# First modulation of a two-block network: weights fetched ahead of the constants, and its last 512 columns computed with the weights as stationary operand

## Chip, cores and metric

The kernel runs on one core of a Trainium2 chip, as one launch. The metric is the device time of that launch in microseconds (us); lower is better. A profile of one execution lists every instruction with its start and length. PE is TensorE's matmul stream, PEld its weight loads, DVE is VectorE, ACT is ScalarE, POOL is GpSimd, SP is SyncE, whose queue issues every DMA here.

## What is computed

A two-layer block (an mLSTM mixer, a gated spatial mixer, a feed-forward network after each), followed by a block with sparse attention, a convolution branch and 16384 small experts, for 256 tokens of width 1024. All of it is float32. The change touches only how the first layer's modulation vectors are made:

```python
c_act = jax.nn.silu(c)                        # c: 1 x 1024
for i in range(DEPTH):
    mod = c_act @ ada_w[i] + ada_b[i]         # 1 x 6144
    sh1, sc1, g1, sh2, sc2, g2 = jnp.split(mod[:, None, :], 6, axis=-1)
    h = rmsnorm(x, norm_g[i, 0]) * (1.0 + sc1) + sh1
    ...                                       # mixer (mLSTM for i = 0), residual, ffn
```

`sh1` and `sc1` of layer 0 are needed before the first projection can start; the other four vectors are made in the background, between other work.

## The kernel before

The program is written for a tile framework: code names tiles and engines, and a scheduler sets the order of each engine's instructions from priorities. Inside an engine's list nothing overtakes. All DMAs are issued by SP, in one list.

`full` calls `setup` and then `first_block`. `setup` (L339) issues three constant loads: `cols` (331 columns of small vectors, `c` among them), `kc` (six 128x128 matrices: identity, ones, masks) and `ciota`; then it makes `cact` = silu(c), 8 columns of 128 values.

`first_block` (L866) first spreads `cact` over 128 columns (`crep`, L871) and makes `sh1` and `sc1` in four blocks of 512 output columns with `ada_start` (L494). A block needs 8 chunks of weights, 128 rows by 512 columns each. They come as four DMAs of 512 KB, two to a staging tile `st` (pool `wst`, three tiles of 1 MB). Even chunks go to PE: `crep[:, kk]` is the stationary operand and the 512 weight columns move (L512), so that all 128 rows of the result are equal. Odd chunks are multiplied and summed on DVE into `s` (L508, L510), and one matmul with the ones matrix (L513) adds that sum over the partitions. `diagonal` (L517) takes the wanted column form out of the 128 equal rows with two DVE operations over 512 columns (L521, L522), L515 adds the bias, and L877 forms (1 + sc1) * gain after the last block. X is fetched behind the first block's weights (L875).

`Finish.whole` (L247) then normalises X (`chain`, L157), transposes it on PE (`turn`, L194, L203), scales it with `sc1` and `sh1` on DVE (L212, first half of the features) and ACT (L216, second half) into `hf`, and runs the heads (L128): the gate weights (40 columns, `a_w_g`) and the first two of the query/key column groups, for each half of the tokens (`t` = 0, 1), with L135. The tiles for these head weights take the room of `crep`. What follows is `mlstm` (L625): six query/key groups with `dense_b` (L407, its matmuls on L397 to L399), meanwhile the gate chain on ACT and DVE (L639 to L661: `th`, `lf`, `C`, `av`, `M`, `em`), then the value projection with `Acc.emit` (L113) from `a_w_v`, and background work from `self.side`: the other modulation vectors by `ada_block` (L524, its DVE steps on L538).

Weights for `dense_b` and `Acc` arrive in float32 and are split: ACT makes `hi` (L365), DVE makes `lo` (L366).

Of the kernel before, what the change touches and what calls it, by code (L numbers as in the profile page):

```python
# [10 lines left out]
F32 = mybir.dt.float32  # L11
# [5 lines left out]
AF = mybir.ActivationFunctionType  # L17
ALU = mybir.AluOpType
# [5 lines left out]
KD = 8  # L24
T = 256
EPS = 1e-6
NEG = -1.0e30
# [248 lines left out]
class Net:  # L276
# [61 lines left out]

    def setup(self):  # L339
        nc, c, a = self.nc, self.const, self.a  # L340
        self.cols = c.tile([128, NCOL], F32, name="cols")
        nc.sync.dma_start(self.cols, a["cols"])
        self.X = self.keep.tile([128, 2, D], F32, name="X")
        k = c.tile([128, 6, 128], F32, name="kc")
        nc.sync.dma_start(k, a["k128"])
        self.junk = self.const.tile([128, D], BF16, name="junk")
        self.ident, self.ones, self.mbig, self.anti, self.bdiag, self.iota = (k[:, i] for i in range(6))
        self.cand_iota = c.tile([128, NCAND], F32, name="ciota")
        nc.sync.dma_start(self.cand_iota, a["ciota"])
        self.mhalf = c.tile([128, 1], F32, name="mhalf")  # L350
        nc.gpsimd.memset(self.mhalf, -0.5)
        self.eps = c.tile([128, 1], F32, name="eps")
        nc.gpsimd.memset(self.eps, EPS)
        self.cact = c.tile([128, KD], F32, name="cact")
        nc.scalar.activation(self.cact, self.col("c"), AF.Silu)

    def col(self, name, i=None, n=1):
        at, w = COLS[name]
# [132 lines left out]
        return t  # L491


    def ada_start(self, i, b, o):  # L494


        nc = self.nc
        s = self.ada_p.tile([128, 1024], F32, tag="ada", name="ada")[:, :512]
        w = self.a["ada_w"][i, b // 2].rearrange("q p (k n) -> q p k n", k=2)[:, :, :, (b % 2) * 512:(b % 2 + 1) * 512]
        ps = self.sd_tile()  # L500
        for h in range(2):
            st = self.wst.tile([128, 2048], F32, tag="st", name="st").rearrange("p (k n) -> p k n", k=4)
            for q in range(2):
                nc.sync.dma_start(st[:, 2 * q:2 * q + 2], w[2 * h + q])
            for k in range(4):
                kk = 4 * h + k
                if kk == 1:
                    nc.vector.tensor_scalar(s, st[:, k], self.cact[:, kk:kk + 1], None, op0=ALU.mult)  # L508
                elif k % 2:
                    nc.vector.scalar_tensor_tensor(s, st[:, k], self.cact[:, kk:kk + 1], s, op0=ALU.mult, op1=ALU.add)  # L510
                else:
                    nc.tensor.matmul(ps, self.crep[:, kk], st[:, k], start=kk == 0, stop=False)  # L512
        nc.tensor.matmul(ps, self.ones, s, start=False, stop=True)  # L513
        self.diagonal(ps, o)
        nc.vector.tensor_tensor(o, o, self.col("ada_b", 48 * i + 4 * b, 4), op=ALU.add)  # L515

    def diagonal(self, ps, o):  # L517

        nc = self.nc
        d = self.ada_p.tile([128, 4, 128], F32, tag="adad", name="adad", bufs=1)  # L520
        nc.vector.tensor_tensor(d, ps.rearrange("p (k c) -> p k c", k=4), self.ident.unsqueeze(1).to_broadcast([128, 4, 128]), op=ALU.mult)  # L521
        nc.vector.tensor_reduce(o, d, axis=AX.X, op=ALU.add)  # L522
# [343 lines left out]
    def first_block(self):  # L866
        with self.tc.tile_pool(name="adap", bufs=2) as self.ada_p, self.tc.tile_pool(name="wsx", bufs=2) as self.wsx:
            m0, first, rest = self.ada_mods(0)
            with self.tc.tile_pool(name="crep", bufs=1) as p:
                self.crep = p.tile([128, KD, 128], F32, name="crep")  # L870
                self.nc.vector.tensor_copy(self.crep, self.cact.unsqueeze(2).to_broadcast([128, KD, 128]))  # L871
                for b in range(4):
                    self.ada_start(0, b, m0["sh1" if b < 2 else "sc1"][:, 4 * (b % 2):4 * (b % 2) + 4])
                    if b == 0:
                        self.nc.sync.dma_start(self.X, self.a["x"].rearrange("o (t p) d -> p (o t) d", p=128))  # L875
                o = m0["sc1"]
                self.nc.vector.scalar_tensor_tensor(o, o, 1.0, self.col("ng0_0"), op0=ALU.add, op1=ALU.mult)  # L877
            with self.tc.tile_pool(name="st0", bufs=2) as p, self.tc.tile_pool(name="work", bufs=1) as work:
                fin = Finish(self, work, None, m0["sc1"], m0["sh1"], head=[(self.a["a_w_g"], 1, 40)] + self.pairs(self.a["a_w_qk"], 2), head_pool=p)
                fin.whole()  # L880
            self.side = rest[:3]
            x = self.mlstm(fin.x, 2.0, lambda p, hst: Finish(self, p, m0["g1"], m0["sc2"], m0["sh2"], head=self.pairs(self.a["ffn_w1"][0], 4), head_pool=hst))
            m1, first, rest1 = self.ada_mods(1)
            with self.tc.tile_pool(name="sgc", bufs=1) as p:
                self.side = rest[3:] + first + [self.sgu_setup(p)]
                with self.tc.tile_pool(name="hst1", bufs=1) as hst:
                    x = self.ffn(x, 0, Finish(self, None, m0["g2"], m1["sc1"], m1["sh1"], head=self.pairs(self.a["b_w_u"], 4), head_pool=Both(hst, self.wst)), 3.2)
                self.side = rest1[:3]

                rows = Lent(self.sgu_c[:2])  # L890
                x = self.sgu(x, 1.2, lambda v: Finish(self, None, m1["g1"], m1["sc2"], m1["sh2"], head=self.pairs(self.a["ffn_w1"][1], 3), head_pool=rows, space=v))
            self.side = rest1[3:]
            with self.tc.tile_pool(name="hst2", bufs=2) as hst:
                x = self.ffn(x, 1, Finish(self, None, m1["g2"], self.col("attn_g"), head=self.pairs(self.a["w_glu"], 3), head_pool=hst), 2.0)
        self.wsx = None
        return x
# [605 lines left out]
def prep(i):  # L1502
    c = lambda v: np.asarray(v).reshape(-1, 128).T
# [9 lines left out]
    for l in range(2):  # L1513
        for j in (0, 2):
            col[f"ng{l}_{j}"] = c(i["norm_g"][l, j])
    o = {}
    o["cols"] = np.concatenate([col[n] for n in COLS], axis=1)
    p, f = np.arange(128)[:, None], np.arange(128)[None, :]
    f32 = np.float32
    o["k128"] = np.stack([  # L1520
        (p == f).astype(f32), np.ones((128, 128), f32), np.where(p > f, f32(-NEG), f32(0)), (p + f == 127).astype(f32),
        (p // 64 == f // 64).astype(f32), np.broadcast_to(f.astype(f32), (128, 128)),
    ], axis=1)
    o["ciota"] = np.broadcast_to(np.arange(NCAND, dtype=f32)[None], (128, NCAND))
# [6 lines left out]
    w = i["a_w_in"][0]  # L1531
# [5 lines left out]
    w = i["b_w_in"][0]  # L1537
# [5 lines left out]
    w = i["w_in_2"][0]  # L1543
# [37 lines left out]
```

## Time and profile before

| | us |
|---|---|
| median of 3 runs | 1751.74 |
| lowest, highest run | 1751.68, 1752.71 |
| profiled execution, its own time | 1752.71 |
| its span, first to last instruction | 1751.0 |
| PE busy in the span | 1713.6 (98%) |

The 1.7 us between the profiled execution's time and its span lie before the first and behind the last instruction. Rows of the timeline give the start, the length, engine, line, operation, tiles and count of a run of equal instructions; in brackets stands how long the engine was idle before them and what ended that idle time. A float32 matmul appears as two records on PE. The next two sections show the change and the rows.

### The profile page before, as it was taken

Reading aid. Unit: us, or ns where it says so; the run is one execution under the profiler, and the core shown is the slowest. Engines: PE = TensorE matmul, PEld = TensorE weight load, DVE = VectorE, ACT = ScalarE, POOL = GpSimd, SP = SyncE. Lnnn points to the kernel's source line nnn. Section 1 sums busy time; section 2 is a strip of 40 time slices with the busy share of each in tenths; the row PEclk is TensorE's granted clock in tenths of the full one; section 3 lists DMA queues with packets and bytes.
Section 4 is the critical chain, followed back from the end, with each engine's and each line's share of the span. In section 5 each row is a group of like instructions: output and inputs, shape, how many; then the busy total and the mean of one; then the engine's idle time right before and its main releaser. Section 6 shows DMA issues by size and latency. Waiting matters only on the chain.

```text
span 1751.0 us, 28455 instructions
## 1 busy us (share of the span) xinstructions
PE 1713.6 (98%) x11306; PEld 1511.8 (86%) x11306; DVE 1382.8 (79%) x2407; ACT 917.0 (52%) x1519; POOL 31.7 (2%) x43
## 2 busy tenths in 40 slices
PE   7999999999999999999999999999999999999998
PEld 3878888877888888999999999999888998787886
DVE  6787996578959655999767999799788948888754
ACT  3565566544546665666555445445444444445543
POOL 0010000000000000000000000000000000000000
PEclk9999999999999999999999999999999999999999
DMA  9876887367818653444355555544554455554751
GB/s 341 307 283 243 332 320 295 121 219 286 309 65 334 211 191 129 152 169 147 119 180 182 174 188 184 178 165 165 177 172 168 167 173 189 176 184 160 258 192 45
DMA packets 59599, 352.42 MB, mean 201 GB/s; under 512 B 6165, under 2 KB 12613, under 8 KB 19273
## 3 DMA queue, kind: packets, MB, share of 16 engines
q1 hardware_dynamic: 59466, 350.61, 56.7%
q8 instruction: 88, 1.44, 0.3%
q14 instruction: 45, 0.37, 0.1%
HBM read 349.51 MB, written 1.07 MB: 200 GB/s over the span
## 4 chain that ended last, share of the span: by engine, by line
PE 85%; DVE 8%; DMA 2%; issue 2%; ACT 2%; POOL 1%; SPq 0%; POOLq 0%; DVEq 0%; ACTq 0%
PE acc L113 38%; PE mm L397 10%; PE mm L399 10%; PE mm L398 10%; PE mm L426 6%; PE mm L428 3%; PE head L135 3%; DVE lo L366 2%; DVE yc L937 1%; DMA st<-in_b_w_v_dram 1%; PE sd L1234 1%; PE sd L1245 1%; DVE ada L538 1%; PE sd L512 1%; DMA st<-in_ada_w_dram 1%
## 5 line engine op out<-in xcount | busy, mean ns | idle before, releaser
L365 ACT CAST hi<-st 128x1024 fp32r<-128x1024 f32 (+1 forms) x507 | 525.9, 1049 | 435.7 <-PE mm L398 196.0
L366 DVE TENSOR_TENSOR lo<-st,hi 128x1024 fp32r<-128x1024 f32 (+1 forms) x507 | 613.1, 1221 | 153.0 <-ACT hi L365 151.2
L397 PE MATMUL mm<-h,hi 128*128 128x256 f32 x1544 | 443.2, 287 | 0.7 <-ACT qz L670 0.7
L399 PE MATMUL mm<-h,lo 128*128 128x256 f32 x1544 | 436.7, 283 | 1.9 <-DVE lo L366 1.9
L398 PE MATMUL mm<-h,hi 128*128 128x256 f32 x1544 | 436.9, 283 | 0.0
L399 PEld LDWEIGHTS mm<-h,lo 128*128 128x128 f32 x1544 | 295.2, 191 | 2.6 <-DVE lo L366 2.6
L397 PEld LDWEIGHTS mm<-h,hi 128*128 128x128 f32 x1544 | 295.4, 191 | 1.9 <-ACT qz L670 0.9
L398 PEld LDWEIGHTS mm<-h,hi 128*128 128x128 f32 x1544 | 295.5, 191 | 0.2
L113 PE MATMUL acc<-hi,h 128*128 128x512 f32 x768 | 232.0, 398 | 6.6 <-ACT hi L365 4.7
L113 PEld LDWEIGHTS acc<-hi,h 128*128 128x128 f32 x768 | 143.1, 190 | 37.9 <-ACT hi L365 6.2
L113 PE MATMUL acc<-lo,h 128*128 128x512 f32 x544 | 172.1, 394 | 0.2
L426 PE MATMUL mm<-h,hi 128*128 128x512 f32 x456 | 161.6, 399 | 0.0
L113 PE MATMUL acc<-hi,vh 128*128 128x512 f32 x448 | 142.5, 399 | 0.0
L113 PE MATMUL acc<-lo,vh 128*128 128x512 f32 x448 | 138.7, 391 | 0.0
L113 PE MATMUL acc<-hi,vl 128*128 128x512 f32 x448 | 138.0, 389 | 0.0
L113 PEld LDWEIGHTS acc<-lo,h 128*128 128x128 f32 x544 | 102.2, 189 | 23.7 <-DVE lo L366 2.5
L428 PE MATMUL mm<-h,lo 128*128 128x256 f32 x399 | 111.9, 281 | 0.0
L113 PEld LDWEIGHTS acc<-hi,vl 128*128 128x128 f32 x448 | 84.1, 188 | 18.4
L113 PEld LDWEIGHTS acc<-lo,vh 128*128 128x128 f32 x448 | 84.1, 188 | 18.1
L538 DVE SCALAR_TENSOR_TENSOR ada<-st,cact,ada 128x1024 f32<-128x1024 f32 x74 | 94.7, 1280 | 5.7 <-DMA st<-in_ada_w_dram 3.3
L113 PE MATMUL acc<-hi,l 128*128 128x512 f32 x320 | 99.0, 389 | 0.0
L426 PEld LDWEIGHTS mm<-h,hi 128*128 128x128 f32 x456 | 83.7, 188 | 16.6 <-issue 0.5
(398 smaller groups left out, 2198.7 us busy)
## 6 DMA issues: line engine op xcount, KB each, us to landing
st<-in_peer_u_dram SPq DMA_DIRECT2D x64, 1024.0 KB, 4.9
st<-in_peer_v_dram SPq DMA_DIRECT2D x64, 1024.0 KB, 4.9
st<-in_ffn_w_dram SPq DMA_DIRECT2D x62, 1024.0 KB, 5.7
st<-in_ada_w_dram SPq DMA_DIRECT2D x40, 1024.0 KB, 6.2
st<-in_ada_w_dram SPq DMA_DIRECT2D x16, 512.0 KB, 6.2
st<-in_b_w_u_dram SPq DMA_DIRECT2D x8, 1024.0 KB, 5.0
st<-in_b_w_v_dram SPq DMA_DIRECT2D x8, 1024.0 KB, 4.9
st<-in_b_w_out_dram SPq DMA_DIRECT2D x8, 1024.0 KB, 5.2
```

Of the source, the lines that this page charges most:

```text
L113: ins = mm(self.t[t][j], a[:, ts], b[:, j * 512:(j + 1) * 512], start=first and a is xh and b is wh, stop=last and a is xl)
L135: net.nc.tensor.matmul(ps[:, t * 128:(t + 1) * 128], w[:, k], x(k), start=k == 0, stop=k == KD - 1)
L365: i = self.nc.scalar.copy(hi, src)
L366: return i.ins, self.nc.vector.tensor_tensor(lo, src, hi.bitcast(F32), op=ALU.subtract).ins
L397: mm(out, ahi, bhi, start=start, stop=False)
L398: mm(out, ahi, blo, start=False, stop=False)
L399: return mm(out, alo, bhi, start=False, stop=stop)
L426: i = mm(ps, wh[:, k], x2[:, k], start=first, stop=last)
L428: i = mm(ps[:, :T], wl[:, k], xh[:, k], start=False, stop=False)
L512: nc.tensor.matmul(ps, self.crep[:, kk], st[:, k], start=kk == 0, stop=False)
L538: nc.vector.scalar_tensor_tensor(s, w, c, s, op0=ALU.mult, op1=ALU.add)
L937: nc.vector.scalar_tensor_tensor(y[:, n], up[:, n, w:w + T], self.col("conv_w", n * 31 + w), y[:, n], op0=ALU.mult, op1=ALU.add)
```

## The change

`setup` now loads only `c` (8 columns, tile `c8`). The identity and ones matrices, X and `cols` are issued by `fetch`, which `ada_start` calls after the first block's first two weight DMAs; the remaining matrices (`kd`, three of them, since an unused one is dropped) and `ciota` are issued by `fetch_more`, after `Finish.whole`. The fourth block goes through the new `ada_last`: its 8 chunks come as eight DMAs of 256 KB, each 128x128 part of a chunk is loaded as stationary operand, and one column of `cact` moves (L545 of the new kernel), 32 matmuls with one column of output each, summed over the chunks in four PSUM tiles; four DVE operations on single columns (L547) add bias and one and multiply by the gain.

```diff
     def setup(self):
         nc, c, a = self.nc, self.const, self.a
+        c8 = c.tile([128, KD], F32, name="c8")
+        nc.sync.dma_start(c8, a["cols"][:, :KD])
         self.cols = c.tile([128, NCOL], F32, name="cols")
-        nc.sync.dma_start(self.cols, a["cols"])
...
+    def fetch(self):
+
+        nc, a = self.nc, self.a
+        nc.sync.dma_start(self.k2, a["k128"][:, :2])
+        nc.sync.dma_start(self.X, a["x"].rearrange("o (t p) d -> p (o t) d", p=128))
+        nc.sync.dma_start(self.cols, a["cols"])
+
+    def fetch_more(self):
+
+        nc, a = self.nc, self.a
+        nc.sync.dma_start(self.k4, a["k128"][:, 2:])
+        nc.sync.dma_start(self.cand_iota, a["ciota"])
...
+            if h == 0:
+                then()
...
+    def ada_last(self, i, b, o, ng):
+
+        nc = self.nc
+        b1 = self.small.tile([128, 4], F32, tag="b1", name="b1", bufs=1)
+        nc.vector.tensor_scalar(b1, self.col("ada_b", 48 * i + 4 * b, 4), 1.0, None, op0=ALU.add)
+        w = self.a["ada_w"][i, b // 2].rearrange("q p (k n) -> q p k n", k=2)[:, :, :, (b % 2) * 512:(b % 2 + 1) * 512]
+        ps = [self.acc_p.tile([128, 512], F32, tag="acc", name="adac")[:, :1] for _ in range(4)]
+        for h in range(2):
+            st = self.wst.tile([128, 2048], F32, tag="st", name="st").rearrange("p (k n) -> p k n", k=4)
+            for k in range(4):
+                kk = 4 * h + k
+                nc.sync.dma_start(st[:, k], w[kk // 2, :, kk % 2])
+                for j in range(4):
+                    nc.tensor.matmul(ps[j], st[:, k, j * 128:(j + 1) * 128], self.cact[:, kk:kk + 1], start=kk == 0, stop=kk == KD - 1)
+        for j in range(4):
+            nc.vector.tensor_scalar(o[:, j:j + 1], ps[j], b1[:, j:j + 1], ng[:, j:j + 1], op0=ALU.add, op1=ALU.mult)
...
-                for b in range(4):
-                    self.ada_start(0, b, m0["sh1" if b < 2 else "sc1"][:, 4 * (b % 2):4 * (b % 2) + 4])
-                    if b == 0:
-                        self.nc.sync.dma_start(self.X, self.a["x"].rearrange("o (t p) d -> p (o t) d", p=128))
-                o = m0["sc1"]
-                self.nc.vector.scalar_tensor_tensor(o, o, 1.0, self.col("ng0_0"), op0=ALU.add, op1=ALU.mult)
+                o, ng = m0["sc1"], self.col("ng0_0")
+                self.ada_start(0, 0, m0["sh1"][:, :4], self.fetch)
+                self.ada_start(0, 1, m0["sh1"][:, 4:])
+                self.ada_start(0, 2, o[:, :4])
+                self.nc.vector.scalar_tensor_tensor(o[:, :4], o[:, :4], 1.0, ng[:, :4], op0=ALU.add, op1=ALU.mult)
+                self.ada_last(0, 3, o[:, 4:], ng[:, 4:])
...
                 fin.whole()
+                self.fetch_more()
```

The order of instructions moves at three places that matter below. The first is SP's list at the start of the program; before:

```order
L342 DMA cols<-in_cols_dram 128x331
L345 DMA kc<-in_k_dram 128x768
L349 DMA ciota<-in_ciota_dram 128x54
L504 DMA st<-in_ada_w_dram 128x2x512 x4
L875 DMA X<-in_x_dram 128x2x1024
L504 DMA st<-in_ada_w_dram 128x2x512 x12
L371 DMA st<-in_a_w_qk_dram 128x2048
L371 DMA st<-in_a_w_g_dram 128x320
```

and after the change, where `c` is `c8` and `kc` holds two matrices:

```order
L342 DMA c_84<-in_cols_dram 128x8
L517 DMA st<-in_ada_w_dram 128x2x512 x2
L360 DMA kc<-in_k_dram 128x256
L361 DMA X<-in_x_dram 128x2x1024
L362 DMA cols<-in_cols_dram 128x331
L517 DMA st<-in_ada_w_dram 128x2x512 x10
L543 DMA st<-in_ada_w_dram 128x512 x8
L384 DMA st<-in_a_w_g_dram 128x320
L384 DMA st<-in_a_w_qk_dram 128x2048
L367 DMA kd<-in_k_dram 128x384
L368 DMA ciota<-in_ciota_dram 128x54
```

One small load and two weight pieces now stand ahead of X, X stands ahead of the third piece, and the head weights follow the last modulation piece directly.

The second place is PE's list from the third block to the heads; before:

```order
L512 MATMUL sd<-st,crep 128x512 x2
L513 MATMUL sd<-ada,kc 128x512
L203 MATMUL sd<-kc,xn 128x128 x4
L135 MATMUL head<-hf,st 40x128 x8
L135 MATMUL head<-hf,st 128x128 x16
L135 MATMUL head<-hf,st 40x128 x8
L135 MATMUL head<-hf,st 128x128 x16
```

and after (L527 and L528 are the former L512 and L513):

```order
L527 MATMUL sd<-st,crep 128x512 x2
L528 MATMUL sd<-ada,kc 128x512
L545 MATMUL adac<-cact,st 128x1 x12
L203 MATMUL sd<-kc,xn 128x128 x4
L545 MATMUL adac<-cact,st 128x1 x20
L135 MATMUL head<-hf,st 40x128 x8
L135 MATMUL head<-hf,st 128x128 x16
L135 MATMUL head<-hf,st 40x128 x8
L135 MATMUL head<-hf,st 128x128 x16
```

The fourth block is now a stretch of 32 one-column matmuls, broken only by four transposes, and the heads follow it with nothing between.

The third place is ACT's list in the first mixer, while the query/key groups run on PE (`qz` takes a query group out of PSUM, `hi` splits the last query/key weights); before:

```order
L365 CAST hi<-st 128x1024 x2
L669 COPY qz<-mm 64x256
L670 COPY qz<-mm 64x256
L662 ACT_TABLE_LOAD
L662 ACTIVATE em<-em 8x256
L672 ACTIVATE kT<-mm 128x256 x2
```

and after:

```order
L694 ACT_TABLE_LOAD
L694 ACTIVATE em<-em 8x256
L701 COPY qz<-mm 64x256
L702 COPY qz<-mm 64x256
L378 CAST hi<-st 128x1024 x2
L704 ACTIVATE kT<-mm 128x256 x3
```

The two casts moved behind `em`. DVE's `lo` of the same weights and two background steps wait behind them, and the tile that those steps free is the one into which the first `a_w_v` weights go. From the end of the first mixer on, the lists of all engines are the same as before.

## Rows read from the trace of the kernel before

**Rows 1.** The page: busy time of each engine, share of the span, instructions.
```profile
PE 1713.6 (98%) x11306; PEld 1511.8 (86%) x11306; DVE 1382.8 (79%) x2407; ACT 917.0 (52%) x1519; POOL 31.7 (2%) x43
```

**Rows 2.** Timeline of the start: start us, length, instruction, count, idle before it.
```profile
0.80 0.39 SPq L342 DMA_DIRECT2D cols<-in_cols_dram  x1
...
2.19 2.61 SPq L504 DMA_DIRECT2D st<-in_ada_w_dram  x4
...
3.41 0.70 DVE L871 COPY crep<-cact 128x1024 f32<-128x1024 f32 x1 [3.41 <-ACT cact L355]
4.83 0.63 SPq L875 DMA_DIRECT2D X<-in_x_dram  x1
...
7.02 6.26 PE L512 MATMUL sd<-st,crep 128*128 128x512 f32 x8 [7.02 <-DMA st<-in_ada_w_dram]
```

**Rows 3.** Busy time by stretch: us, engines, granted clock, DMA share, GB/s.
```profile
6.00:20.00 14.00, 10.72 (x21) 4.40 (x22) 7.55 (x14) 3.28 (x9) 1.64 (x2) 1.00 1.04 393
20.00:24.00 4.00, 3.70 (x9) 1.44 (x8) 2.83 (x7) 0.00 (x0) 0.00 (x0) 1.00 0.98 318
```

**Rows 4.** Timeline: third block's last matmul, then the end of the fourth block.
```profile
26.02 1.02 PE L513 MATMUL sd<-ada,kc 128*128 128x512 f32 x2
...
30.73 0.75 DVE L510 SCALAR_TENSOR_TENSOR ada<-st,cact,ada 128x512 f32<-128x512 f32 x1 [0.44 <-DMA st<-in_ada_w_dram]
...
32.70 0.69 DVE L521 TENSOR_TENSOR adad<-sd,kc 128x512 f32<-128x512 f32 x1 [1.22 <-PE sd L513]
...
34.55 2.90 ACT L216 ACTIVATE hf<-mm,sh,sc 128x128 f32<-128x128 f32 x8 [5.21 <-DVE sc L877]
```

**Rows 5.** Timeline of the heads and the first query/key matmul behind them.
```profile
35.02 13.26 PE L135 MATMUL head<-hf,st 128*40 128x128 f32 x96 [0.91 <-DVE hf L212]
...
38.15 6.10 PEld L135 LDWEIGHTS head<-hf,st 128*128 128x128 f32 x48 [0.37 <-issue]
...
44.44 3.65 PEld L135 LDWEIGHTS head<-hf,st 128*128 128x128 f32 x32 [0.19 <-issue]
...
48.03 0.36 PE L397 MATMUL mm<-h,hi 128*128 128x256 f32 x1
```

**Rows 6.** Single lines: ns minimum/median/maximum of a record, first and last start.
```profile
L953 PEld LDWEIGHTS sd<-kc,qi x16: 186/192/192, 852.1 to 853.8; 128*128 128x128 f32 x16
L953 PE MATMUL sd<-kc,qi x16: 250/250/271, 852.1 to 853.8; 128*128 128x1 f32 x16
...
L963 PEld LDWEIGHTS sd<-dg,kc x4: 285/333/333, 855.4 to 856.0; 128*128 128x128 f32 x4
...
L512 PE MATMUL sd<-st,crep x32: 592/593/1191, 7.0 to 31.2; 128*128 128x512 f32 x32
```

**Rows 7.** Busy time by stretch around two falls of the granted clock.
```profile
32.80:36.10 3.30, 1.74 (x11) 1.00 (x12) 3.16 (x9) 1.55 (x5) 0.00 (x0) 1.00 0.96 325
36.20:39.50 3.30, 3.30 (x16) 2.77 (x15) 2.50 (x7) 3.30 (x9) 0.00 (x0) 0.50 0.93 390
...
851.90:855.30 3.40, 3.30 (x28) 3.04 (x27) 0.82 (x4) 1.19 (x2) 0.70 (x1) 1.00 0.20 84
855.40:858.70 3.30, 3.30 (x15) 3.30 (x16) 2.87 (x5) 1.28 (x1) 0.00 (x0) 0.50 0.02 5
```

**Rows 8.** First mixer: issue with its landing (KB, us), then timeline rows.
```profile
st<-in_a_w_v_dram SPq DMA_DIRECT2D x1, 1024.0 KB, 4.9
...
56.96 0.34 SPq L371 DMA_DIRECT2D st<-in_a_w_v_dram  x1
...
57.45 1.28 ACT L662 ACT_TABLE_LOAD   x1
...
66.82 0.63 PE L113 MATMUL acc<-hi,h 128*128 128x512 f32 x2
73.00 0.73 PE L113 MATMUL acc<-hi,h 128*128 128x512 f32 x2 [0.55 <-ACT hi L365]
...
116.50 0.70 PE L695 MATMUL sd<-qz,kT 128*128 128x256 f32 x2 [1.50 <-DVE sh L550]
```

More of the change, by code (lines that the diff above doesn't have):

```diff
@@ L340, in setup @@
         nc, c, a = self.nc, self.const, self.a
+        c8 = c.tile([128, KD], F32, name="c8")
+        nc.sync.dma_start(c8, a["cols"][:, :KD])
         self.cols = c.tile([128, NCOL], F32, name="cols")
-        nc.sync.dma_start(self.cols, a["cols"])
         self.X = self.keep.tile([128, 2, D], F32, name="X")
-        k = c.tile([128, 6, 128], F32, name="kc")
-        nc.sync.dma_start(k, a["k128"])
+        self.k2, self.k4 = c.tile([128, 2, 128], F32, name="kc"), c.tile([128, 3, 128], F32, name="kd")
         self.junk = self.const.tile([128, D], BF16, name="junk")
-        self.ident, self.ones, self.mbig, self.anti, self.bdiag, self.iota = (k[:, i] for i in range(6))
+        self.ident, self.ones = (self.k2[:, i] for i in range(2))
+        self.mbig, self.bdiag, self.iota = (self.k4[:, i] for i in range(3))
         self.cand_iota = c.tile([128, NCAND], F32, name="ciota")
-        nc.sync.dma_start(self.cand_iota, a["ciota"])
         self.mhalf = c.tile([128, 1], F32, name="mhalf")
@@ L354, in setup @@
         self.cact = c.tile([128, KD], F32, name="cact")
-        nc.scalar.activation(self.cact, self.col("c"), AF.Silu)
+        nc.scalar.activation(self.cact, c8, AF.Silu)
+    def fetch(self):
[7 more added lines that the diff above has]
+        nc.sync.dma_start(self.cand_iota, a["ciota"])
     def col(self, name, i=None, n=1):
@@ L491, in bcast_row, with ada_start @@
         return t
-    def ada_start(self, i, b, o):
+    def ada_start(self, i, b, o, then=lambda: None):
         nc = self.nc
@@ L1520, in prep @@
     o["k128"] = np.stack([
-        (p == f).astype(f32), np.ones((128, 128), f32), np.where(p > f, f32(-NEG), f32(0)), (p + f == 127).astype(f32),
+        (p == f).astype(f32), np.ones((128, 128), f32), np.where(p > f, f32(-NEG), f32(0)),
         (p // 64 == f // 64).astype(f32), np.broadcast_to(f.astype(f32), (128, 128)),
```

## Prediction

> **What bounds the kernel now.** I read the page's busy times first: PE is 98% busy over the span [rows 1], so a change of 1% of the time has to be sought where PE waits. The timeline of the start shows one such place. PE's first matmul comes at 7.02, released by a weight DMA [rows 2], and until the features `hf` start at 34.55 the program makes one modulation after the other at the speed of the weight stream: 393 GB/s with the DMA engines full from 6 to 20, 318 GB/s from 20 to 24 [rows 3]. In the tail of the fourth block the reader should see a chain on two engines: the last piece is used at 30.73, PE's ones matmul has ended at 32.70, and DVE's diagonal, bias and gain end at 34.5 [rows 4]. From 35.0 PE is filled: heads until 48.03 (I call this moment H: the first `dense_b` matmul), then query/key groups until 66.82, then `a_w_v` [rows 5, 8]. Instruction order behind the first mixer does not change, so what the change is worth is how far H moves, plus what the first mixer adds or gives back.
>
> **The stream starts earlier: a gain.** Ahead of the first 512 KB piece stood 165.5, 384 and 27 KB of constants; it was issued at 2.19 and used at 7.02 [rows 2], 4.8 later. Now only `c8` is ahead, and one issue takes about 0.45 (the 0.39 of the first one and the gap behind it), so the piece is issued at 1.25. On an idle queue 1024 KB landed 4.9 after their issue [rows 8]; at 393 GB/s they need 2.7, so 2.2 is fixed, and 512 KB need 2.2 + 1.3 = 3.5. It lands at 4.8, 2.2 earlier; if it still takes 4.8, at 6.0, 1.0 earlier. I take 2.1, since the constants that it waited for are gone. `crep` took until 4.1 [rows 2] and its source now lands first, so it isn't late. Against that the identity and ones matrices (128 KB) and `cols` (165.5 KB), which went through before the stream was full, are now inside it: 0.30 MB at 393 GB/s, 0.8. Net -1.3 (ends -0.2 and -1.3).
>
> X now stands ahead of pieces 3 and 4: PE has two pieces early, then waits some 2 us, and works longer at the half clock of the start, where a 512-column record took up to 1191 ns against 593 [rows 6]. Its staging tiles come free later, which is what the 318 GB/s stretch shows today [rows 3]. I price it at +0.4, between 0 and 1.0 (the whole 20 to 24 dip is worth (393 - 318)/393 x 4 = 0.8). Before, PE was through the third block at 26.02 + 2 x 0.43 = 26.9, with 0.43 the spacing of full-clock records in that block. Now it is at S = 26.9 - 1.3 + 0.4 = 26.0, ends 25.6 and 27.7.
>
> **The fourth block: from the DMA's pace to PE's.** Removed are four 512-column matmuls, the ones matmul, DVE's four multiplies and the diagonal: from the use of the last piece at 30.73 to the features at 34.55, 3.8 of chain [rows 4]. Put in their place are 32 one-column matmuls, 64 records, each with its own 128x128 float32 weight load, and four transposes stand among them: 68 records. The trace has this form once: L953, one column, 16 records between 852.1 and 853.8 [rows 6], (853.8 - 852.1)/15 = 0.113 each. So the stretch needs 68 x 0.113 = 7.7 of PE at full clock, while the last DMA lands around 29: PE, not the stream, now sets the end. At full clock it ends at E = 26.0 + 7.7 = 33.7; with 0.4 for the drain and DVE's small operations `sc1` is ready at 34.1. The 3.8 of chain that went away buys 0.4.
>
> **The clock is the term that decides.** The granted clock fell from 2.4 to 1.2 GHz at 36.1, 3.4 after the last dense matmuls had ended [rows 4, 7], and again at 855.3, 3.2 after L953 began; in that stretch PE and PEld were both filled (3.30 and 3.04 of 3.40), and L953 made up 1.8 of it [rows 6, 7]. So one-column matmuls did not hold the clock there, although PE looked busy. In the new version they last over 7 us, and I expect the fall 3.3 after S (I allow 2 to 5; two cases are no rule). At half clock 16 head records took 3.30 [rows 7], 0.21 each, and a weight load 333 ns against 192 [rows 6]; I price the one-column records at 0.21 there. By the fall 3.3/0.113 = 29 records are done; 39 x 0.21 = 8.2 remain: E = 26.0 + 3.3 + 8.2 = 37.5. A fall after 2 gives 38.7, after 5 36.0.
>
> **From E to H.** The heads start at half clock. Both stays at half clock above lasted 3.4 [rows 7], and at the start it took about 5 (eight records in 6.26 instead of 8 x 0.43) [rows 2]; I take 4.3 of dense heads until it rises. 16 records of 40 columns at 0.21 are 3.4 (the first four chunks no longer wait for `sc1`, ACT brings the others in time at 2.90/8 = 0.36 each [rows 4]); 4 more records at 0.21; then 28 + 16 + 32 at full clock, 0.112 each (3.65 for 32 [rows 5]), 8.5. H = E + 12.8 = 50.3, against 48.03: +2.3, ends +0.5 and +3.9 with the fall and the rise alone. The head weights are not in the way: they were issued late before (heads went on at 38.15 [rows 5]), now directly behind the last piece, and land around 32. `fetch_more` is 219 KB on a queue that then has slack; I price it at nothing, and 0.6 (219 KB at 393 GB/s) if it delays the weights behind it.
>
> **The first mixer.** In ACT's list the two `hi` casts of the last query/key weights now stand behind the table load (1.28 [rows 8]) and `em`. By ACT's times before, they end near H + 11; DVE's two `lo` and two background steps behind them end near H + 14.9, and only then the first `a_w_v` can be issued. It was issued at 56.96, H + 8.9; with 4.9 to landing and 1.05 for its cast PE gets it at H + 20.9, where it wants it at 66.82 = H + 18.8 [rows 8]: 2.1 of waiting. The 0.55 that PE waited for the second piece at 73.00 goes. Later PE waits 1.50 for DVE at 116.50 [rows 8], which can absorb part. I take +1.0, ends 0 and +2.0.
>
> Sum: +2.3 + 1.0 = +3.3 on the profiled execution, 1752.7 + 3.3 = 1756.0. That execution lay 1.0 above the median of 1751.7, so the median becomes 1755.0.
>
> **A rule against the trace.** The clock terms above rest on the load's 333 ns at half clock against 192. The Trainium skill (TensorE: Matmul & The Clock Gate, section "LDWEIGHTS (loading the stationary operand)") gives a load's time as its columns divided by 1.2, in ns, 107 for 128 columns, with no term for the clock's state. The 0.113 at full clock agrees; at half clock the rows speak against it. By that page the one-column stretch would not slow down at all, which is the second rival.
>
> **Rivals.** (1) Slower: the clock falls early, 2 after S, and the `a_w_v` wait comes in full. E = 38.7, H = 51.5, +3.5; +2.0 in the mixer: +5.5, 1757.2. It decides if the fall comes within about 2.5 of the start of the one-column stretch. For it: the transposes and DMA-paced matmuls before S are not dense either. Against: the two falls came 3.2 and 3.4 after.
> (2) Loads don't slow at half clock. E = 33.7, the heads still begin at half clock, H = 46.5, -1.5; with +1.0 in the mixer -0.5: 1751.2. Against: 333 ns against 192.
> (3) Faster: weight loads hold the clock. E = 33.7; the last four 40-column chunks wait for ACT until E + 2.3; then 80 records at 0.112, 9.0: H = 45.0, -3.0; +1.0: -2.0, 1749.7, or 1748.7 if the mixer adds nothing. Against: the fall at 855.3 with PEld filled.
>
> **How the numbers follow.** Forecast 0.48 (1755.0, its own range 1752.8 to 1757.2); rival 1 0.25; rival 2 0.17; rival 3 0.10. A measurement of this kernel tells 0.2%, 3.5 us, from no change. Slower by more: most of rival 1 (0.21) and the upper third of the forecast (0.14), 0.35. Faster by more: the low end of rival 3 and of the stream's start, 0.08. The rest, 0.57, is within. The range reaches from rival 3 to the upper end of rival 1 with S late: 1749.0 to 1758.5.
>
> **What would show it.** In the profile of the changed kernel the first matmul stands near 5; the third block's last matmul ends near 26; L545 then runs at 0.11 a record with the DMA ahead of it and, some 3 us in, at 0.21, with the granted clock at 0.50 from there into the heads; the first `dense_b` matmul stands near 50; PE waits some 2 us before its first `a_w_v` matmul. If L545 keeps 0.11 to its end, rivals 2 or 3 hold, told apart by the clock column. If S is off by more than 1.5, the stream's start was mis-priced.

## Result and profile after

| | before | after |
|---|---|---|
| median, us | 1752.71 | 1762.23 |
| lowest, highest run | 1751.68, 1755.13 | 1761.51, 1766.09 |
| span of the profiled execution | 1751.0 | 1760.5 |

The ratio after to before is 1.0061, with a 95% interval of 1.0046 to 1.0076: the change costs 0.6%. It went the way that was forecast, but the time lies 3.7 above the upper end of the range. The kernel of before has 1752.71 over the five runs made beside the changed one; the three runs of its own section had 1751.74.

The page's row of busy times, against [rows 1]: PE is busy 7.7 longer, and its waits grow by 1.8. Busy time grows at half clock too, as the table by stretch below shows.

```profile
PE 1721.3 (98%) x11360; PEld 1522.9 (87%) x11360; DVE 1381.1 (78%) x2405; ACT 917.2 (52%) x1519; POOL 32.7 (2%) x43
```

The timeline of the start of the changed kernel, which answers to [rows 2, 4, 5]:

```profile
1.25 1.29 SPq L517 DMA_DIRECT2D st<-in_ada_w_dram  x2
...
6.22 3.75 PE L527 MATMUL sd<-st,crep 128*128 128x512 f32 x4 [6.22 <-DMA st<-in_ada_w_dram]
...
12.25 2.08 PE L527 MATMUL sd<-st,crep 128*128 128x512 f32 x2 [2.28 <-DMA st<-in_ada_w_dram]
...
22.66 0.66 PE L203 MATMUL sd<-kc,xn 128*128 128x128 f32 x4
...
27.71 1.02 PE L528 MATMUL sd<-ada,kc 128*128 128x512 f32 x2
...
28.57 2.73 PE L545 MATMUL adac<-cact,st 128*128 128x1 f32 x24
...
31.64 7.88 PE L545 MATMUL adac<-cact,st 128*128 128x1 f32 x40
...
39.45 12.87 PE L135 MATMUL head<-hf,st 128*40 128x128 f32 x96
...
52.07 0.36 PE L410 MATMUL mm<-h,hi 128*128 128x256 f32 x1
```

The first matmul is 0.8 earlier, but behind two pieces PE waits 2.28 for the third. The one-column stretch takes 24 records in 2.73 and then 40 in 7.88. The table by stretch says why (us, PE, PEld, DVE, ACT, POOL, granted clock, DMA share, GB/s):

```profile
28.50:32.30 3.80, 3.80 (x36) 3.73 (x34) 3.07 (x8) 0.00 (x0) 0.00 (x0) 1.00 1.04 386
32.40:39.40 7.00, 7.00 (x34) 7.00 (x33) 0.82 (x3) 0.81 (x2) 0.00 (x0) 0.50 1.01 400
39.50:42.50 3.00, 3.00 (x16) 2.67 (x16) 1.79 (x6) 3.00 (x8) 0.00 (x0) 0.50 0.83 273
...
71.00:74.30 3.30, 0.07 (x2) 0.04 (x1) 0.99 (x2) 3.30 (x9) 0.00 (x0) 0.85 1.01 410
74.30:80.10 5.80, 5.80 (x14) 4.54 (x15) 5.76 (x5) 2.85 (x3) 0.00 (x0) 0.50 0.65 233
```

From 32.35 to 42.59 the granted clock was 0.50 with PE and PEld filled: 34 records in 7.00, 0.206 each, against 0.114 (24 records in 2.73) ahead of it. The last two rows are the second loss: PE idle from 71.03, then half clock (0.50 from 73.31 to 80.14). The timeline of the mixer, which answers to [rows 8], shows what PE waited for:

```profile
59.15 0.36 SPq L384 DMA_DIRECT2D st<-in_ada_w_dram  x1
...
62.27 1.22 DVE L379 TENSOR_TENSOR lo<-st,hi 128x1024 fp32r<-128x1024 f32 x1 [3.12 <-ACT hi L378]
63.41 1.28 DVE L570 SCALAR_TENSOR_TENSOR ada<-st,cact,ada 128x1024 f32<-128x1024 f32 x1
64.61 1.22 DVE L379 TENSOR_TENSOR lo<-st,hi 128x1024 fp32r<-128x1024 f32 x1
...
65.85 0.35 SPq L384 DMA_DIRECT2D st<-in_a_w_v_dram  x1
...
70.83 1.31 ACT L724 ACTIVATE e<-mx,ac 128x256 f32<-128x256 f32 x3 [2.25 <-DVE mx L691]
...
73.18 1.98 ACT L378 CAST hi<-st 128x1024 fp32r<-128x1024 f32 x2
...
74.27 2.08 PE L113 MATMUL acc<-hi,h 128*128 128x512 f32 x4 [3.23 <-ACT hi L378]
...
145.22 1.94 PE L497 MATMUL sd<-kc,og 128*128 128x128 f32 x8 [3.45 <-DVE og L781]
```

The same place in the kernel before, DVE's list around the `lo` steps and PE's wait for `og`:

```profile
53.88 1.27 DVE L538 SCALAR_TENSOR_TENSOR ada<-st,cact,ada 128x1024 f32<-128x1024 f32 x1
...
55.68 1.25 DVE L538 SCALAR_TENSOR_TENSOR ada<-st,cact,ada 128x1024 f32<-128x1024 f32 x1
...
57.19 2.34 DVE L366 TENSOR_TENSOR lo<-st,hi 128x1024 fp32r<-128x1024 f32 x2
...
134.09 1.06 PE L484 MATMUL sd<-kc,og 128*128 128x128 f32 x8 [1.35 <-DVE og L749]
```

The first `a_w_v` load was issued at 65.85, 13.8 after H (8.9 before the change), right behind the second `lo`, which freed its tile at 65.83; a background piece, which had stood behind it, was issued ahead of it at 59.15. Before, two background multiplies (L538, L570 in the changed kernel) stood ahead of the `lo` steps, and the load went right behind the second of them. Now DVE idles 3.12 until ACT's `hi` at 62.27, and a multiply stands between the two `lo`. Later PE waits 3.45 for `og` where it had waited 1.35, and the granted clock is 0.50 from 144.99 to 148.41.

Where the time came from is read off the starts of the same instruction in both traces:

| PE instruction | before | after | later by |
|---|---|---|---|
| first 512-column matmul | 7.02 | 6.22 | -0.80 |
| ones matmul of the second block | 20.59 | 20.75 | +0.16 |
| ones matmul of the third block | 26.02 | 27.71 | +1.69 |
| first `dense_b` matmul (H) | 48.03 | 52.07 | +4.04 |
| first `a_w_v` matmul | 66.82 | 74.27 | +7.45 |
| ones matmul of the background block behind it | 78.92 | 88.01 | +9.09 |
| transposes of `og` | 134.09 | 145.22 | +11.13 |
| behind the first mixer | 165.59 | 177.76 | +12.17 |
| same instruction, behind the stay near 374 | 411.70 | 421.94 | +10.24 |
| same instruction, behind the stay near 855 | 892.57 | 902.04 | +9.47 |
| near the end | 1733.73 | 1743.15 | +9.42 |

Start and heads cost 4.0, the first mixer 8.1. The 2.7 that come back later are two stays at half clock: the one at 374 lasted 6.8 before and 3.4 after (there it begins at 387), and the one at 855 is missing after. The second profile of the kernel before, below, lacks the one at 855 too, and its instructions stand 0.9 earlier from there on, so that this is no doing of the change. What sets the length of the other is open: it is 6.8 in both profiles of the kernel before and in e1, e4 and e6 below, 3.4 in the others.

### The profile page after: what moved, and what is told of

Its sections match the earlier page's. It is cut to its first block, busy times and chain, and to the rows that moved or that the text cites. A ratio compares the mean times of both kernels' runs of the same rounds, so it can differ in the third digit from the quotient of the medians.

```text
span 1760.5 us, 28566 instructions
## 1 busy us (share of the span) xinstructions
PE 1721.3 (98%) x11360; PEld 1522.9 (87%) x11360; DVE 1381.1 (78%) x2405; ACT 917.2 (52%) x1519; POOL 32.7 (2%) x43
## 4 chain that ended last, share of the span: by engine, by line
PE 86%; DVE 7%; ACT 2%; issue 2%; DMA 1%; POOL 1%; SPq 0%; POOLq 0%; DVEq 0%; ACTq 0%
PE acc L113 39%; PE mm L410 10%; PE mm L412 9%; PE mm L411 9%; PE mm L439 6%; PE mm L441 3%; PE head L135 2%; DVE lo L379 2%; DVE yc L970 1%; PE sd L1267 1%; PE sd L1278 1%; DMA st<-in_ada_w_dram 1%; DVE ada L570 1%; ACT hi L378 1%; POOL rs_r L470 1%
## 5 line engine op out<-in xcount | busy, mean ns | idle before, releaser
L570 DVE SCALAR_TENSOR_TENSOR ada<-st,cact,ada 128x1024 f32<-128x1024 f32 x74 | 94.8, 1282 | 2.5 <-DMA st<-in_ada_w_dram 1.2
```

Source lines behind the costliest of these rows:

```text
L570: nc.vector.scalar_tensor_tensor(s, w, c, s, op0=ALU.mult, op1=ALU.add)
```

## Experiments

The theory after the result has three parts: the fetch order at the start, the clock in the one-column stretch, and the order of the lists in the first mixer. The rivals are that the fetch order carries the loss alone, and that the late start makes the value weights late whatever the lists say.

| | ratio to before, 95% interval | S | H | S to H | longest PE wait, H to 85 |
|---|---|---|---|---|---|
| after | 1.0061 (1.0046 to 1.0076) | 28.57 | 52.07 | 23.50 | 3.23 |
| e1 fetch order alone | 0.9999 (0.9990 to 1.0008) | | 49.15 | | 0.67 |
| e2 fourth block alone | 1.0042 (1.0028 to 1.0055) | 27.99 | 51.45 | 23.46 | 1.41 |
| e3 after, 128 columns | 1.0030 (1.0018 to 1.0043) | 28.62 | 48.93 | 20.31 | 3.71 |
| e4 after, ACT's list back | 1.0068 (1.0054 to 1.0081) | 29.75 | 53.21 | 23.46 | 5.15 |
| e5 after, four lists back | 1.0029 (1.0017 to 1.0042) | 28.37 | 51.83 | 23.46 | 1.92 |
| e6 e5 with 128 columns | 1.0032 (1.0020 to 1.0044) | 27.85 | 48.16 | 20.31 | 2.75 |
| e7 e6 with X later | 1.0015 (1.0006 to 1.0024) | 27.77 | 48.08 | 20.31 | 2.75 |
| e8 e6 with the old fetch | 1.0015 (1.0006 to 1.0024) | 29.35 | 49.66 | 20.31 | 2.74 |
| e9 after, SP's and DVE's lists back | 1.0026 (1.0016 to 1.0037) | 28.77 | 53.86 | 25.09 | 1.41 |
| e10 after, SP's and ACT's lists back | 1.0053 (1.0039 to 1.0067) | 30.46 | 53.92 | 23.46 | 3.91 |
| e11 e7 with one step freed | 1.0013 (1.0004 to 1.0022) | 27.97 | 48.28 | 20.31 | 2.83 |

S is the start of the fourth block's matmuls, H the first `dense_b` matmul; all times are in us.

**e1: the fetch order alone.**

```diff
-                self.nc.vector.scalar_tensor_tensor(o[:, :4], o[:, :4], 1.0, ng[:, :4], op0=ALU.add, op1=ALU.mult)
-                self.ada_last(0, 3, o[:, 4:], ng[:, 4:])
+                self.ada_start(0, 3, o[:, 4:])
+                self.nc.vector.scalar_tensor_tensor(o, o, 1.0, ng, op0=ALU.add, op1=ALU.mult)
```

> Only the new fetch order (c8 first, two weight pieces, then constants and X); the fourth block is made as before the change. Theory (the loss has three parts: start of the stream, clock in the one-column stretch, list order in the first mixer): the third block ends near 28.6 as in the changed kernel, the features start about 1.7 later than before the change, near 36.2, the first dense_b matmul stands near 49.7 and nothing is lost in the mixer, where the lists read as before the change: +1.0 to +2.5, about 1754.5. Rival (the fetch order carries the loss, by X ahead of the third piece and the longer half clock at the start): first dense_b matmul near 52, and +4 or more.

Measured: 1752.65 us, ratio 0.9999, below the +1.0 to +2.5 that I gave. The heads start at 36.30 in place of 35.02, H is 1.1 later, and the mixer adds nothing. The timeline of e1:

```profile
5.53 3.75 PE L527 MATMUL sd<-st,crep 128*128 128x512 f32 x4 [5.53 <-DMA st<-in_ada_w_dram]
12.56 1.76 PE L527 MATMUL sd<-st,crep 128*128 128x512 f32 x2 [3.29 <-DMA st<-in_ada_w_dram]
...
27.35 1.02 PE L528 MATMUL sd<-ada,kc 128*128 128x512 f32 x2
```

PE begins 1.5 earlier, then has nothing for 3.29 while X goes through, and is 1.3 later at the third block's end. In the time the order is worth nothing, within the interval of 0.1%, and it doesn't carry the loss.

**e2: the new fourth block alone**, in the kernel of before.

```diff
-                for b in range(4):
+                for b in range(3):
...
+                self.ada_last(0, 3, o[:, 4:], ng[:, 4:])
```

> Only the new fourth block (32 one-column matmuls, eight DMAs of 256 KB); setup, constants and X are fetched as before the change. Theory: the third block ends at 26.9, the granted clock falls 3 to 4 later, the stretch ends near 37.9, first dense_b matmul near 50.5 (+2.4); SP's list has the first a_w_v load behind a background piece and the two mx loads, so PE waits 2 to 3.5 for it and then runs at half clock: +7 to +8.5, about 1760. Rival (the fetch order carries the loss): first dense_b matmul at 48 to 49, total within 2 of the time before.

Measured: 1759.75 us, ratio 1.0042, as expected in the sum. S is 27.99 and not 26.9: in the new PE list two groups of four transposes, 0.49 each, stand ahead of S that stood behind it before. H is 3.4 later. The stretches of e2:

```profile
28.00:33.20 5.20, 5.20 (x49) 5.20 (x48) 3.08 (x8) 0.00 (x0) 0.00 (x0) 1.00 1.06 415
33.40:37.40 4.00, 4.00 (x20) 4.00 (x19) 0.80 (x3) 0.79 (x2) 0.00 (x0) 0.50 1.02 418
```

The clock falls 5.3 after S. In the mixer PE waits 1.41 for `a_w_v`, less than expected, and later 3.47 for `og`. Most of the loss, 0.42% of 0.61%, is the fourth block with what it does to the lists; the remaining 0.19% is within what the two intervals allow.

**e3: 128 moving columns.**

```diff
...
-nc.tensor.matmul(ps[j], st[:, k, j * 128:(j + 1) * 128], self.cact[:, kk:kk + 1], start=kk == 0, stop=kk == KD - 1)
+nc.tensor.matmul(ps[j], st[:, k, j * 128:(j + 1) * 128], self.cact[:, kk:kk + 1].to_broadcast([128, 128]), start=kk == 0, stop=kk == KD - 1)
...
```

> The changed kernel with 128 moving columns (the same column of cact 128 times) in place of one, in the same 32 matmuls; column 0 of each result is used. Theory (one-column matmuls let the clock fall, 128 columns hold it at the same 0.113 a record): the third block ends near 28.6, the stretch takes 7.7 and ends near 36.3 with the granted clock at 1.00 throughout, first dense_b matmul near 47.6, 4.5 earlier than with one column; the mixer keeps its loss of some 5: about 1757.5. Rival (weight loads set the clock whatever moves, or loads wait for DMA): the stretch ends near 39.5 at 0.50 as in the changed kernel, about 1762.

Measured: 1757.59 us, ratio 1.0030, as expected in the sum; H is 1.3 later than I gave. The stretches of e3, and its line L545 (ns minimum/median/maximum), with the loads of the changed kernel last:

```profile
28.60:32.30 3.70, 3.70 (x34) 3.68 (x33) 3.07 (x8) 0.00 (x0) 0.00 (x0) 1.00 1.09 408
32.40:35.80 3.40, 3.40 (x32) 3.33 (x30) 0.51 (x3) 0.19 (x1) 0.00 (x0) 1.00 1.03 406
```

```profile
L545 PEld LDWEIGHTS adac<-cact,st x64: 190/191/192, 28.2 to 35.5; 128*128 128x128 f32 x64
L545 PE MATMUL adac<-cact,st x64: 273/273/275, 28.6 to 35.7; 128*128 128x128 f32 x64
```

```profile
L545 PEld LDWEIGHTS adac<-cact,st x64: 190/312/338, 28.1 to 39.1; 128*128 128x128 f32 x64
```

The same 64 records with 128 columns in place of one take 7.31, 0.114 each, and the clock stays at 1.00. That settles the clock part: in all six traces with one column the clock fell, 2.3 to 5.3 after S; in none of the five with 128 columns did it fall between S and H. From S to H it takes 23.46 to 23.50 against 20.31, 3.2 us (25.09 in e9, where the fall came at 2.3). PE's list is not quite the same in the two: with 128 columns the four transposes stand between the two halves of the heads. The mixer's loss needs no late H: H is only 0.9 later than before here, yet the first `a_w_v` load goes 13.8 after H again, PE waits 3.71, and the transposes of `og` stand at 141.96, 7.9 later than before.

**e4: ACT's list in the mixer put back**: `em` behind the two `hi` casts, the exponentials `e` behind the casts of the first value weights.

```diff
-            nc.scalar.activation(em, em, AF.Exp)
...
+                    w3 = self.weights_b(a["a_w_qk"][3])
+                    with self.tc.issue_after(self.hi):
+                        nc.scalar.activation(em, em, AF.Exp)
...
+                with self.tc.issue_after(hi0):
+                    nc.scalar.activation(e[:, :T], mx[:, h, :T], AF.Exp, bias=ac[:, 0, h:h + 1], scale=-1.0)
```

> The changed kernel with ACT's list in the first mixer put back: em behind the two hi casts of the last query/key weights, the decay exponentials e behind the hi casts of the first a_w_v weights; SP then has the first a_w_v load ahead of the mx loads and of the next background piece, as before the change. Theory (list order costs 5 in the mixer): first dense_b matmul at 52.07 as in the changed kernel, PE waits under 1 before the first a_w_v matmul, the granted clock stays at 1.00 there, total +4 to +5 against before: about 1756.7. Rival (the wait follows from the late start and not from the lists): 3 of waiting stays, about 1762.

Measured: 1763.98 us, ratio 1.0068. My theory missed. The timeline of e4:

```profile
72.00 0.63 PE L113 MATMUL acc<-hi,h 128*128 128x512 f32 x2
...
74.29 7.88 DVE L571 SCALAR_TENSOR_TENSOR ada<-st,cact,ada 128x1024 f32<-128x1024 f32 x6
...
82.78 1.22 PE L113 MATMUL acc<-hi,h 128*128 128x512 f32 x2 [5.15 <-ACT hi L378]
```

The first piece comes in time, and PE goes on at 72.00 without a wait. The wait moved to the second piece, 5.15, since DVE's list now has all six background multiplies behind the `mx` steps, and they hold the staging tiles. So with ACT's list back, and SP's order with it, the first piece is in time, but the scheduler wrote another list for DVE, and the total did not fall. ACT's list alone is not the cause of the loss that I took it for.

**e5: the four lists put back.** The first 32, 72, 112 and 520 instructions of the mixer on SP, ACT, DVE and PE get an edge each to the one ahead of them in the order of before, which fixes the order and waits for nothing.

```diff
+ORDER = {
+    "SP": "34 98 167 172 176 170 238 411 19 246 21-22 280 284 318 322 339 343 401 434 496 516 578 598 662 1319 682 806 840 844 848 852",
...
+                        self.tc.add_manual_dep(i, last.name, info, reason="order")
```

> The changed kernel with the lists of SP, ACT, DVE and PE in the first mixer (32, 72, 112 and 520 instructions from its start) tied to the order that they had before the change; start, fetch order and one-column matmuls as changed. Theory (the change of the lists costs 5 in the mixer, by staging tiles that go to a background piece ahead of the value weights): first dense_b matmul near 52, 4.0 to 5 later than before, and from there on nothing more is lost: PE waits under 1 for the first two value-weight pieces, the granted clock stays at 1.00 from the heads to the end of the mixer, +4 to +5, about 1757. Rival (the late start makes the value weights late whatever the lists): a wait of 3 or more for the first or second piece stays, then half clock, 1760 to 1764.

Measured: 1756.78 us, ratio 1.0029, in the sum as the theory had it. The timeline of e5:

```profile
57.68 1.27 DVE L578 SCALAR_TENSOR_TENSOR ada<-st,cact,ada 128x1024 f32<-128x1024 f32 x1
...
59.47 1.25 DVE L578 SCALAR_TENSOR_TENSOR ada<-st,cact,ada 128x1024 f32<-128x1024 f32 x1
...
60.75 0.33 SPq L392 DMA_DIRECT2D st<-in_a_w_v_dram  x1
60.99 2.34 DVE L387 TENSOR_TENSOR lo<-st,hi 128x1024 fp32r<-128x1024 f32 x2
...
78.17 1.20 PE L113 MATMUL acc<-hi,h 128*128 128x512 f32 x4 [1.92 <-ACT hi L386]
```

The two background multiplies end at 60.72, ahead of the `lo` steps, and the value weights go at 60.75, 8.9 after H, as before the change. One wait of 1.92 is left, where I had under 1, with no fall of the clock behind it; PE is 3.8 late at H, 5.2 at 87, and stays at 5.1 to 5.2 to the end of the mixer. With the one-column matmuls kept, the lists cost 0.3%, about 5 us.

**e9 and e10: which list.** e9 ties SP and DVE to the old order and ACT to the new one as far as `em` and the casts; e10 ties SP and ACT to the old order and leaves DVE free. PE's list is free in both. Of the edits, e9's row for ACT:

```diff
+ORDER = {
...
+    "ACT": "37 41 101 105 8 10 29 11 30 31 32 68 69 27 95 96 179 183 132 158",
...
```

> The changed kernel; in the first mixer SP's and DVE's lists are tied to the order of before the change, and ACT's list is tied to the new order as far as em and the two hi casts (em first). Theory (what frees the staging tile for the first value weights is DVE's two background multiplies, which stood ahead of the lo steps and now stand between and behind them): first a_w_v load issued near 61 to 62, first a_w_v matmul within 1 of the last query/key matmul, total +3.5 to +5, about 1757. Rival (the two hi casts behind em on ACT decide, as the prediction had it): load issued near 66, 2 to 3.5 of waiting, then half clock, 1760 or more.

> The mirror of it: SP's and ACT's lists as before the change, DVE's list left free, so that its background multiplies stand between and behind the two lo steps as in the changed kernel. Theory (DVE's list decides): load issued near 64 to 65, a wait for the first or the second piece of 1 to 4, total 1758 to 1762. Rival (ACT's list decides): no wait above 1, about 1757.

Measured: 1757.78 us (1.0026) and 1762.28 us (1.0053). The timeline of e9, then that of e10:

```profile
61.51 1.25 DVE L577 SCALAR_TENSOR_TENSOR ada<-st,cact,ada 128x1024 f32<-128x1024 f32 x1
...
62.78 0.34 SPq L391 DMA_DIRECT2D st<-in_a_w_v_dram  x1
...
80.14 1.20 PE L113 MATMUL acc<-hi,h 128*128 128x512 f32 x4 [1.41 <-ACT hi L385]
```

```profile
62.77 1.28 DVE L576 SCALAR_TENSOR_TENSOR ada<-st,cact,ada 128x1024 f32<-128x1024 f32 x1
63.96 1.22 DVE L385 TENSOR_TENSOR lo<-st,hi 128x1024 fp32r<-128x1024 f32 x1
...
65.21 0.34 SPq L390 DMA_DIRECT2D st<-in_a_w_v_dram  x1
...
82.51 0.88 PE L113 MATMUL acc<-hi,h 128*128 128x512 f32 x2 [3.91 <-ACT hi L384]
```

With nearly the same H (53.86 and 53.92), the load goes 8.9 after H where DVE's multiplies stand first, although ACT has `em` ahead of the casts, and 11.3 after H where they stand between the `lo` steps. The totals go the same way: e9 is with e5 (1.0026, 1.0029), e10 near the changed kernel (1.0053, 1.0061). So DVE's list decides, SP's being the same in both; no run changes SP's list alone. ACT's list, with SP's that came back with it, bears on the first piece: in e10, as in e4, `hi` is not late, DVE idles 0.62 before the first `lo` in place of 3.12, and the first `a_w_v` matmul stands at 72.98, 19.1 after H (18.8 before the change, 22.2 in the changed kernel); it is the second piece that PE then waits 3.91 for. e9's issue came a little later than the 61 to 62 I gave only because its clock fell early and H with it.

**e6, e7, e8, e11: is there a version that beats both?** e6 is e5 with the edit of e3. e7 also moves X and the constants behind the fourth piece. e8 has the fetch order of before. e11 is e7 with DVE's step `b`, the bias of the gate activation `th`, let off its place. The edit that e7 adds:

```diff
-            if h == 0:
+            if h == 1:
                 then()
```

> The same with 128 moving columns in the fourth block. Theory (three separate causes: clock in the one-column stretch, mixer lists, start): both losses go, first dense_b matmul near 48.9, total +0.5 to +1.5, about 1753.5. Rival: 2 or more of waiting in the mixer stay, 1756 or more.

> The same again, and the matrices, X and cols issued behind the first block's fourth weight piece, not its second. Theory (X ahead of the third piece leaves PE without weights for 2.3 to 3.6 near 10, and so holds the staging tiles longer): no such wait, third block ends near 26.7, first dense_b matmul near 47, total -0.5 to -1.5, about 1751.5. Rival (the same bytes stand ahead of the third block's end wherever X is): third block's end within 0.5 of 28.6, total as the run without this edit, about 1753.5.

> Only the new fourth block, with 128 moving columns and the mixer lists of before the change; fetch order of before the change. Theory: third block's end at 27 to 28 as with the one-column version of this, no fall of the clock, first dense_b matmul 47.2 to 48.3, total -0.8 to +0.3, about 1752.3. With the run that has the new fetch order as well it shows what fetching the weights ahead of the constants is worth by itself: theory, nothing to 1 us.

> 128 moving columns, X and the constants behind the fourth weight piece, and the mixer lists of before the change except DVE's small step b (the bias of the gate activation th), which may go ahead of the four lo steps. Theory (the 2.75 of waiting at 54 came from b: th waited for it on ACT, and the query copies behind th held PSUM): that wait falls to under 1, first dense_b matmul near 48, total -0.5 to +1.5, about 1753. Rival (ACT itself is full there): 2 or more stay, about 1756.

Measured: 1757.75, 1755.88, 1755.67 and 1755.02 us; ratios 1.0032, 1.0015, 1.0015, 1.0013. H came within 0.8 of what was expected in e6 and e11, 1.1 later in e7, and 1.4 behind the upper end in e8; the totals are 2.0 to 4.4 above what I gave. The timeline of e6 shows the new wait, and that of e11 what became of it:

```profile
44.96 4.62 DVE L387 TENSOR_TENSOR lo<-st,hi 128x1024 fp32r<-128x1024 f32 x4
...
50.58 0.09 DVE L679 TENSOR_SCALAR b<-cols 40x1 f32<-40x1 f32 x1
...
50.77 0.47 ACT L681 ACTIVATE th<-head,b 40x256 f32<-40x256 f32 x1 [3.17 <-issue]
...
56.90 0.39 PE L418 MATMUL mm<-h,hi 128*128 128x256 f32 x1 [2.75 <-ACT qz L710]
```

```profile
54.93 0.39 PE L418 MATMUL mm<-h,hi 128*128 128x256 f32 x1 [0.66 <-ACT qz L710]
...
75.54 1.21 PE L113 MATMUL acc<-hi,h 128*128 128x512 f32 x4 [2.83 <-ACT hi L386]
```

In e6 `b` stands behind four `lo` steps, `th` waits for it, the query copies behind `th` hold PSUM, and PE waits 2.75. Freed in e11, that wait is 0.66, and 2.83 turn up at the second value-weight piece. The rows give the reason, though no run tested it alone: before, the features were begun 13.5 ahead of H, both halves together, and DVE was through with the four `lo` at 45.1; in e11 the second half starts at 41.4 and the last `lo` ends at 51.0, so that the background loads behind it, and the value weights behind those, meet in the queue: the first `a_w_v` load took 7.5 from issue to landing there, 4.9 before [rows 8]. X's place shows too little to tell: S is 27.85 in e6, 27.77 in e7, 27.97 in e11. The new fetch order gains nothing here either: 1.0032 and 1.0015 with it (e6, e7), 1.0015 with the old one (e8). The gains of e3 and e5 don't add: either edit alone brings the ratio to 1.0030 or 1.0029, both together (e6) leave it at 1.0032, since H is 3.7 earlier than in e5, but the new wait of 2.75, with half clock from 57.51 to 60.93 behind it, takes that back: the first `a_w_v` matmul stands at 70.53 in e6 and at 70.62 in e5. None of these beats the kernel of before.

**e12: the kernel of before once more**, one run, for its start.

> The kernel of before the change once more, for a second profile of its start. Theory (the end of the third block moves by over 1 between executions with the same fetch): it ends anywhere from 26.5 to 29.5, against 26.9 in the first profile. Rival (the start repeats): within 0.3 of 26.9.

Measured: 1751.77 us. The timeline of e12:

```profile
25.46 1.02 PE L513 MATMUL sd<-ada,kc 128*128 128x512 f32 x2
```

The third block ends 0.6 earlier than in the first profile, outside the range that I gave and beyond the 0.3 of the rival, and H, 48.05, is the same to 0.02. The start of before repeats better than I thought, and my theory falls. The starts of the other kernels spread more, S from 27.85 to 30.46 in seven traces with X behind two pieces, and 27.99 and 29.35 in e2 and e8 with the old fetch; what makes them spread is not settled.

## Why the prediction was wrong, and where it was right

**The start: mis-sized.** The first piece was used 4.1 to 5.0 after its issue and not 3.5, so the gain was 0.8 here and 1.3 to 1.6 in seven other traces with this fetch, not 2.1. The wait behind X was seen, but priced at 0.4, and it took the whole gain: +0.16 at the second block's end. And the step that gave S left out two groups of transposes that the new PE list has ahead of it, 1.0 us (e2). S was 28.57, beyond the end of 27.7.

**The one-column stretch and the clock: right.** The full-clock pitch was 0.114 (0.113 forecast), the fall came 3.8 after S (3.3, ends 2 and 5), the half-clock pitch was 0.206 (0.21), E to H 12.6 (12.8). S to H took 23.5 where the sum had 24.3. What the clock costs was too large between forecast and rival 3: 50.3 less 45.0 is 5.3, and the runs show 3.2, since at full clock S to H takes 20.3 and not 19.0. S was 2.6 late and S to H 0.8 short, so H came at 52.07 and not at 50.3.

**The first mixer: the step that failed.** "I take +1.0, ends 0 and +2.0" became +8.1. That the first value-weight load goes late was right, at H + 13.8 where I had H + 14.9. Three things were wrong in it. The cause: I put it on ACT's casts behind `em` and had both background multiplies behind the `lo` steps. The casts did hold DVE for 3.12, but with ACT's list back (e4, e10) the second piece came late instead of the first and the loss stayed, while with SP's and DVE's lists back and ACT's left (e9) most of it went: it hangs on where DVE's background multiplies stand. The size: the wait was 3.23, not 2.1. ACT made six exponentials (70.83 to 73.18) right ahead of the cast; but in e3 they were done at 70.14, and the cast waited until 70.49 for the load, 7.8 after its issue and not 4.9, with 3.71 of waiting on PE. How much of the 3.23 is the exponentials and how much the load is therefore open. And what follows a wait had no price: the clock fell, and the next stretch took 13.74 in place of 12.10; then the lists lost another 3.1 by the mixer's end, most of it at `og` (3.45 of waiting in place of 1.35, with 3.4 at half clock behind it). I expected the later waits to absorb, and the end of +2.0 was the wait itself, no bound on what lies behind it. With the four lists put back (e5), the mixer costs 1.4 of the 8.1.

**Behind the mixer**: -2.7, which the sum did not have; 0.9 of it the kernel of before shows between its own two profiles.

**The rivals.** Rival 1 had the right sign and the full wait, but its trigger, an early fall, did not happen (3.8). Rival 2 falls: in the changed kernel the loads took 190 ns at the least and 338 at the most. The Trainium skill (TensorE: Matmul & The Clock Gate, section "LDWEIGHTS (loading the stationary operand)") gives the columns divided by 1.2, 107 ns for 128 columns, with no term for the clock; the pitch of 0.114 at full clock is near it (a load's own record lasts 190 to 192 there), that of 0.206 at half clock is not, and the measurement decides. Rival 3 falls too: with one column moving, filled weight loads held the clock in none of six traces.

## What to carry over

A record with one moving column took PE 0.113 to 0.114 here, as much as one with 128, and the clock fell 2.3 to 5.3 after a stretch of them began; moving the same column 128 times kept the clock, at the same pitch. Before a step is priced by its own chain, look at what its timing does to a list that a scheduler writes: here an edit of the first 40 us rewrote the lists of four engines up to the end of the first mixer, near 156 before the change, and that cost more than the step itself (8.1 in the mixer, 1.4 with the old lists, against 4.0 at H). A wait of PE's like the 3.23 here is to be priced with the half-clock stretch that follows it, and bytes that are only put in another order ahead of the same last piece saved nothing.

## What the runs showed of the hardware

One moving column and 128 moving columns have the same pitch at full clock (0.114 and 0.114 a record), with the same 190 to 192 ns loads, and yet only the first let the clock fall, in six traces of six against none of five. What follows a wait was less regular: after 3.23, 3.71, 3.91 and 5.15 of idle PE the clock was 0.50 for 3.4 to 6.8; after 1.41 and 1.92 it stayed at 1.00; after 2.74 to 2.75 it fell in e6, e7 and e8, and after 2.83 it did not in e11. A wait of 3.47 at 374.60 in the kernel of before went with 6.8 of half clock, and one of 3.46 at 387.01 in the changed kernel with 3.4.
